# A state-space layer in a fixed instruction order: the kernel transpose moved to the front of a round, tables behind late copies, the next modulation in the first four rounds, gate products in the last two

## The chip, the cores and the metric

One core of one Trainium2 chip runs the whole program. The metric is device time in microseconds of one execution, lower is better. Engines are named as the profile names them: PE (TensorE matmuls), DVE (VectorE), ACT (ScalarE), POOL (GpSimd) and SP (SyncE, which issues the DMA transfers here).

## The reference

A trunk of two residual layers over 512 tokens of width 1024, float32. Layer 0 mixes tokens by a grouped state-space layer (S5), layer 1 by attention with forget gates; a gated convolutional MLP follows each. Every part is modulated by shift, scale and gate from a conditioning vector c. The change touches only the state-space layer:

```python
u = h @ w_in                                  # h: normed, scaled and shifted x
# 64 groups of 16 channels, 64 complex states each, discretised with lam, dt
# scan over time: state = lb * state + bb @ u
y = einsum(hs_re, cr) - einsum(hs_im, ci) + d_skip * u
y = gelu(y)
y = y * sigmoid(y @ w_glu)
return y @ w_out
# the layer's own modulation and the next one's:
shift, scale, gate = split(silu(c) @ ada_w + ada_b, 3)
```

## The kernel before

Weights and activations are float32, and each large product is done as three products of rounded parts (hi by hi, hi by lo, lo by hi). The high part is a copy into a rounded type on ACT (`w_hi`, `a_hi`), the low part a subtraction on POOL or DVE (`w_lo`, `a_lo`, `x_lo`).

The state-space layer is written in method `s5`, in which all engines keep the order of the code: what is written first is issued first on its engine, and an engine that waits holds up all that stands behind it on that engine. There are eight tiles m of 128 channels (8 groups). Time is cut into blocks of 8 steps: inside a block a small convolution kernel does the work, between blocks a scan over 64 blocks. A start stage makes parameters, the scale and shift and the inputs of tiles 0 and 1; then comes a loop of eight rounds. Round m has these steps; the line is that of the kernel before:

- `s5_scan`: 32 small products of `w1` and `u` on PE (L1053), then nine DVE steps with the decay `cf` (made on ACT, L1059) and the turning tables `s_rot`, to the states `ua` (L1081).
- `s5_tables`: POOL builds parts of `s_rot` for later tiles (L966 to L968).
- `s5_columns` of tile m+1: PE products with `dd`, `x` and `s_cd` (L1008, L1011), ACT copies the kernel out as `ktt` (L1016), PE transposes x into `w1` (L1022, copied by ACT at L1023), then PE transposes `ktt` (L1026, "the kernel transpose") and ACT copies it as `kt` (L1027).
- `s5_shifted`: `kt` is stored to DRAM as `s_z` (L1028) and loaded back in shifted form as `tw` (L1037); ACT masks it in eight copies to `t` (L1041).
- `inputs(m+2)`: 24 products on PE (L323), copied by ACT as `uf` (L1313), stored as `s_ud` (L1260) and loaded back turned as `u` (L1264).
- `s5_outputs`: PE products of `u` and `t` (L1091) and of `ua` and `w` (L1100), which ACT sends through a gelu as `yg` (L1106); SP stores it as `s_yd` (L1107). For the gate y is read back as `yt` (L1113), copied by ACT as `a_hi` (L1340), and its low part is `a_lo` (L1344).
- `s5_made`, `s5_states_out`: DVE multiplications (L976) and a POOL addition (L980) that make `x` for tile m+2 and `w` for tile m+1.
- `parted`, `rested`: ACT's high part (L1136) and POOL's low part (L1142) of the input weights of later tiles, loaded as `raw` three at a time.
- `ada_step`: products of c with modulation weights of the next part (L1161), eight steps in all; `ada_columns` (L165, L170) turns their result `ada_rows` into columns. Rows of the layer's own gate are loaded as `ada_raw` and summed on DVE (L265).

In the last two rounds the products of the first four gate tiles (`glu_head`, L1366) stand between these steps; their weights are loaded (`gate_load`), copied (`gate_hi`, L1352) and subtracted (`gate_lo`, L1357) from round 5 on. A fifth gate tile follows, then a loop over the remaining three and `w_out`.

## Time and profile before

| | us |
|---|---|
| median of three runs | 1209.37 |
| the three runs | 1209.37, 1211.93, 1202.32 |
| the profiled execution | 1203.8 |
| its span in the trace | 1201.9 |
| PE, DVE, ACT, POOL busy | 1165.8, 950.2, 649.6, 206.7 |

The span is what the trace covers from the first to the last instruction; the profiled execution took 1.9 us more. PE is busy for 97% of the span. A busy PE is not the same as PE at its best: the trace also gives the clock that TensorE was granted, 1.00 being full speed, and a product takes twice as long at 0.50. In rows of the timeline the number after the start is the duration; matmuls overlap a little, so the distance between two starts is the better measure of what a row takes. In waits, a row says which engine, tile and line waited for which, for how long in total, how often and the longest.

### The profile page before, as it was taken

The numbers are of one execution on the slowest core, as the hardware profiler recorded it, in microseconds if no ns is written. First come the engines' busy times: TensorE is split into PE (matmuls) and PEld (weight loads), VectorE is DVE, ScalarE is ACT, GpSimd is POOL, SyncE is SP. The second block draws the span as 40 slices with busy tenths as digits, with TensorE's granted clock in tenths as the row PEclk, the third lists the DMA queues.
The fourth block names the chain that finished last, engine by engine and source line by source line (L and its number), as shares of the span: only waits on it lengthen the run. The fifth ranks groups of instructions, "written<-read, shape, count | busy, mean of one in ns | idle before, by whom it ended". The sixth has DMA issues, their size and how long they took to land.

```text
span 1201.9 us, 21406 instructions
## 1 busy us (share of the span) xinstructions
PE 1165.8 (97%) x8255; PEld 1038.7 (86%) x8255; DVE 950.2 (79%) x1726; ACT 649.6 (54%) x1169; POOL 206.7 (17%) x266
## 2 busy tenths in 40 slices
PE   7998989999999999999999999999999999999997
PEld 2677767799999999999899788878999999999987
DVE  8865775879898798877676788876899888888855
ACT  3644533435676576666543566664466555555543
POOL 5776540000011111111000433330000000000000
PEclk9898979999999999999999999999999999999999
DMA  9677447853598898998603655622223332333331
GB/s 358 241 244 242 159 151 264 302 171 107 145 249 233 230 255 230 253 239 228 194 25 127 221 180 164 198 97 73 70 87 95 110 126 86 110 124 92 106 88 71
DMA packets 79719, 202.74 MB, mean 169 GB/s; under 512 B 23952, under 2 KB 26480, under 8 KB 78592
## 3 DMA queue, kind: packets, MB, share of 16 engines
q1 hardware_dynamic: 73135, 181.96, 45.1%
q0 software_dynamic: 6192, 18.88, 9.1%
q8 instruction: 65, 1.06, 0.4%
q10 hardware_dynamic: 288, 0.52, 0.1%
q14 instruction: 39, 0.31, 0.1%
HBM read 194.41 MB, written 6.92 MB: 168 GB/s over the span
## 4 chain that ended last, share of the span: by engine, by line
PE 76%; DVE 10%; DMA 6%; ACT 3%; issue 2%; POOL 1%; SPq 0%; DVEq 0%; ACTq 0%; POOLq 0%
PE mmp L323 40%; PE mmp L583 15%; PE aux L583 6%; PE mmp L1582 3%; DMA raw<-in_w_up 2%; DVE w_lo L307 2%; PE aux L1728 2%; PE aux L1711 1%; PE aux L1100 1%; PE aux L1091 1%; DVE ada_raw L265 1%; DVE sums L554 1%; PE aux L1681 1%; DMA yt<-s_yd 1%; DMA raw<-in_s_w_in 1%
## 5 line engine op out<-in xcount | busy, mean ns | idle before, releaser
L302 ACT ACTIVATE w_hi<-raw 128x1024 fp32r<-128x1024 f32 (+4 forms) x196 | 172.1, 887 | 128.6 <-PE mmp L323 55.2
L307 DVE TENSOR_TENSOR w_lo<-raw,w_hi 128x1024 fp32r<-128x1024 f32 (+4 forms) x153 | 155.1, 1016 | 33.0 <-ACT w_hi L302 26.1
L323 PE MATMUL mmp<-ghi,w_hi 128*128 128x512 f32 (+1 forms) x392 | 144.1, 368 | 0.0
L323 PE MATMUL mmp<-glo,w_hi 128*128 128x512 f32 (+1 forms) x392 | 143.7, 367 | 0.0
L323 PE MATMUL mmp<-ghi,w_lo 128*128 128x512 f32 (+1 forms) x392 | 143.6, 366 | 0.0
L323 PE MATMUL mmp<-a_hi,w_hi 128*128 128x256 f32 (+1 forms) x440 | 141.1, 323 | 1.1 <-ACT nm_t L1494 1.1
L323 PE MATMUL mmp<-a_hi,w_lo 128*128 128x256 f32 (+1 forms) x440 | 139.0, 317 | 0.0
L323 PE MATMUL mmp<-a_lo,w_hi 128*128 128x256 f32 (+1 forms) x440 | 138.8, 316 | 0.0
L583 PE MATMUL mmp<-w_hi 128*128 128x256 f32 x420 | 116.6, 278 | 1.6 <-ACT nm_h L590 1.4
L583 PE MATMUL mmp<-w_hi,w_lo 128*128 128x256 f32 x420 | 116.0, 276 | 0.0
L583 PE MATMUL mmp<-w_lo,w_hi 128*128 128x256 f32 x420 | 116.0, 276 | 0.0
L302 ACT ACTIVATE w_hi<-sums 128x1024 fp32r<-128x1024 f32 x78 | 81.8, 1058 | 47.9 <-DVE sums L554 32.3
L307 DVE TENSOR_TENSOR w_lo<-sums,w_hi 128x1024 fp32r<-128x1024 f32 x78 | 94.3, 1218 | 3.1 <-ACT w_hi L302 2.0
L323 PEld LDWEIGHTS mmp<-a_hi,w_hi 128*128 128x128 f32 x440 | 82.2, 188 | 8.6 <-issue 2.5
L265 DVE CUSTOM_DVE_ANT_0 ada_raw<-ada_raw,ada_c,rest 128x1024 f32<-128x1024 f32 x64 | 84.0, 1327 | 5.9 <-DMA ada_raw<-in_ada_rows 5.9
L323 PEld LDWEIGHTS mmp<-a_hi,w_lo 128*128 128x128 f32 x440 | 82.6, 188 | 6.4
L323 PEld LDWEIGHTS mmp<-a_lo,w_hi 128*128 128x128 f32 x440 | 82.8, 188 | 4.6
L323 PEld LDWEIGHTS mmp<-ghi,w_lo 128*128 128x128 f32 x392 | 73.6, 188 | 12.3
L323 PEld LDWEIGHTS mmp<-ghi,w_hi 128*128 128x128 f32 x392 | 73.6, 188 | 11.2
L323 PEld LDWEIGHTS mmp<-glo,w_hi 128*128 128x128 f32 x392 | 73.6, 188 | 11.1
L583 PEld LDWEIGHTS mmp<-w_hi 128*128 128x128 f32 x420 | 78.8, 188 | 2.7 <-ACT nm_h L590 2.7
L554 DVE TENSOR_TENSOR sums<-raw 128x512 f32<-128x512 f32 x70 | 46.0, 686 | 41.5 <-DMA raw<-in_w_up 41.4
(336 smaller groups left out, 3220.9 us busy)
## 6 DMA issues: line engine op xcount, KB each, us to landing
raw<-in_w_up SPq DMA_DIRECT2D x88, 512.0 KB, 3.7
ada_raw<-in_ada_rows SPq DMA_DIRECT2D x64, 512.0 KB, 4.7
raw<-in_ada_w SPq DMA_DIRECT2D x32, 512.0 KB, 6.2
raw<-in_w_down SPq DMA_DIRECT2D x32, 384.0 KB, 4.0
raw<-in_w_down SPq DMA_DIRECT2D x32, 320.0 KB, 3.4
nf<-nfd SPq DMA_DIRECT2D x8, 1152.0 KB, 5.7
w_lo<-in_w_up POOLq DMA_DIRECT2D x17, 512.0 KB, 8.0
raw<-in_fox_qk SPq DMA_DIRECT2D x16, 512.0 KB, 3.3
```

The source lines that it names most:

```text
L265: nc.vector.tensor_tensor_reduce(w, w, self.crow, 1.0, self.ada_b[:, i, m:m + 1], ALU.mult, ALU.add, self.par[i][:, m:m + 1])
L302: nc.scalar.activation(hi, src, AF.Copy)
L307: self.late = (nc.vector.tensor_tensor(lo, src, hi.bitcast(F32), ALU.subtract).ins,)
L323: self.last_mm = self.nc.tensor.matmul(o, wt, xt[:, cols], start=(k == 0 and n == 0), stop=(k == nk - 1 and n == 2),)
L554: sub = lambda o, u, v, op=ALU.subtract: nc.vector.tensor_tensor(o, u, v, op)
L583: self.last_mm = nc.tensor.matmul(o, wt[:, k], xt[:, k], start=(first and k == 0 and n == 0), stop=(k == H - 1 and n == 2), skip_group_che ...
L1091: nc.tensor.matmul(yp[g2][:, k, :], t[:, 2 * k + g2], u[:, g, :], start=(k == 0), stop=False, skip_group_check=True,)
L1100: nc.tensor.matmul(yp[g2][:, k, 1:], w2[rows, k, r].rearrange("p c i -> p (c i)"), st[rows, r, k, :B - 1], start=False, stop=(r == 1), til ...
L1582: self.last_mm = nc.tensor.matmul(ps[q, b][:, :n], xt[:, k, tb], wt, start=(k == 0 and i == 0), stop=(k == KT - 1 and i == 2),)
L1681: nc.tensor.matmul(ps[b][r], q[i][a, tq], kk[j][a, :N], start=(n == 0), stop=(n == 2), tile_position=(64 * r, 0), skip_group_check=True,)
L1711: nc.tensor.transpose(pt[:, r - rs[0], k, :], s[:, r, k * P:(k + 1) * P], self.ident)
L1728: nc.tensor.matmul(pv[:, c * P:], self.v[:, hp, k, r].rearrange("p t d -> p (t d)"), pp[:, r, c + 3 * k:NB + 3 * k, :].rearrange("p b t -> ...
```

## The change

The order of the layer's code is written anew; no product is added or removed.

- Start: the input weights of tile 1 are loaded into a room of `w_hi` ahead of the last modulation loads, and their parts made at once; the columns of tile 0 go ahead of the products with the shift; the states' addition of tile 0 and the low part of w_in(2) go from POOL to DVE; the last of tile 0's tables is built behind them.
- A round: the kernel transpose stands directly behind the columns, ahead of a modulation step and the inputs; `kt` and `tw` are issued ahead of the `u` transfers; `cf` (now `s5_decay`) and `t` of the next tile are made at the end of the round before.
- The eight modulation steps are done in rounds 0 to 3; a row of the gate's modulation is loaded and summed in each of rounds 1 to 4; `ada_columns` moves from round 5 to the tail.
- Last two rounds: the gate products are regrouped (`glu_in`): 12 high-by-high ones in round 6, 36 in round 7. Gate weights are loaded from round 4 on. The low parts of y go to POOL, those of gate tiles 2, 3 and 4 to DVE. The fifth gate tile's products all come last.

```diff
             for m in range(KT):
-                sts[m] = self.s5_scan(m, ws.pop(m), us[m])
+                sts[m] = self.s5_scan(m, ws.pop(m), us[m], cfs.pop(m))
                 next(sts[m])
-                ts[m] = next(ts[m])
...
+                if more:
+                    columns_in(m + 1)
+                    next(cols[m + 1])
...
+                if 0 < m < 4:
+                    ada_step()
+                if m + 4 < KT:
+                    load_w(m + 4)
...
+                if more:
                     ts[m + 1] = self.s5_shifted(m + 1)
                     next(ts[m + 1])
+                if m and m + 2 < KT:
+                    inputs(m + 2)
+                if m + 2 < KT:
+                    turn_u(m + 2)
...
                 outs[m] = self.s5_outputs(m, us.pop(m), ts.pop(m))
                 next(outs[m])
                 outs[m].send((w2s.pop(m), sts.pop(m)))
                 if m + 4 < KT:
                     parted(m + 4)
...
+                if more:
+                    cfs[m + 1] = self.s5_decay(m + 1)
+                    ts[m + 1] = next(ts[m + 1])
                 if steps:
                     ada_step()
```

```diff
+            def glu_in(k, m, j):
+                if m not in gps:
+                    gps[m] = self.mm.tile([P, S], F32, name="mmp")
+                nc.tensor.matmul(gps[m], hi[m][:, k], (yhi, ylo)[j][:, k], start=(k == 0 and j == 0), stop=False)
...
             fifth = [(hi[HEAD][:, k], lo[HEAD][:, k]) for k in range(KT)]
-            for k in range(KT - 1):
-                self.mms(gps[HEAD], fifth, (yhi, ylo), k, KT, full)
             for p in range(2):
                 glu_head(KT - 1, p)
-            self.mms(gps[HEAD], fifth, (yhi, ylo), KT - 1, KT, full)
+            for k in range(KT):
+                self.mms(gps[HEAD], fifth, (yhi, ylo), k, KT, full)
```

Three places show how instructions move. First PE in a round, from the inputs of one round to those of the next. In the kernel before the outputs of round 3 follow the kernel transpose:

```order
L323 MATMUL mmp<-a_xhi,w_lo 128x512
L1026 MATMUL aux<-rest,ktt 128x128
L1091 MATMUL aux<-u,t 128x64 x8
L1100 MATMUL aux<-ua,w_1196 128x63 x16
L1161 MATMUL mmp<-raw,sc_85 32x512 x4
L1053 MATMUL aux<-u,w_1264 64x64 x16
L1008 MATMUL aux<-dd,rest 128x128
L1011 MATMUL aux<-x,s_cd_133 32x128 x8
L1022 MATMUL aux<-rest,x 128x128 x8
L323 MATMUL mmp<-a_xhi,w_hi 128x512
```

In the changed kernel, at the outputs of round 3 as well (lines shift by 1 to 9; L1025 is the kernel transpose, L1062 the scan, L1094 and L1103 the outputs, L1164 a modulation step):

```order
L1094 MATMUL aux<-u,t 128x64 x8
L1103 MATMUL aux<-ua,w_1220 128x63 x16
L1164 MATMUL mmp<-raw,sc_85 32x512 x4
L1062 MATMUL aux<-u,w_1275 64x64 x16
L1007 MATMUL aux<-dd,rest 128x128
L1010 MATMUL aux<-x,s_cd_133 32x128 x8
L1021 MATMUL aux<-rest,x 128x128 x8
L1025 MATMUL aux<-rest,ktt 128x128
```

The kernel transpose has moved from behind the 24 input products to ahead of them. ACT's order around it has stayed: `yg`, `w_hi`, `cf`, `t`, `ktt`, then the copies of `w1`; only `kt` and `uf` behind them have changed places.

Second, SP in a round. Before, in round 4, the `u` transfers of tile 6 come first:

```order
L1260 DMA s_ud<-uf 128x512
L1264 DMA u<-s_ud 128x8x64
L1028 DMA s_z<-kt 128x128
L1037 DMA tw<-s_z 128x1024
L1107 DMA s_yd<-yg 128x8x64
```

In the changed kernel, round 3:

```order
L1027 DMA s_z<-kt 128x128
L193 DMA raw<-in_s_w_in 128x1024
L1036 DMA tw<-s_z 128x1024
L1267 DMA s_ud<-uf 128x512
L1271 DMA u<-s_ud 128x8x64
L258 DMA ada_raw<-in_ada_rows 128x1024
L1110 DMA s_yd<-yg 128x8x64
```

`kt` and `tw` now stand ahead of `uf`'s store and the load that waits for it; a weight load and a modulation row have come in between.

Third, PE in the last two rounds of the changed kernel, from the outputs of round 5 (L1369 are gate products written by `glu_in`):

```order
L1103 MATMUL aux<-ua,w_1554 128x63 x16
L1062 MATMUL aux<-u,w_1616 64x64 x16
L1007 MATMUL aux<-dd,rest 128x128
L1010 MATMUL aux<-x,s_cd_133 32x128 x8
L1021 MATMUL aux<-rest,x 128x128 x8
L1025 MATMUL aux<-rest,ktt 128x128
L1369 MATMUL mmp<-a_hi,w_hi 128x512 x12
L1094 MATMUL aux<-u,t 128x64 x8
L1103 MATMUL aux<-ua,w_1740 128x63 x16
L1062 MATMUL aux<-u,w_1786 64x64 x16
L1369 MATMUL mmp<-a_hi,w_hi 128x512 x4
L1369 MATMUL mmp<-a_lo,w_hi 128x512 x16
```

Before, there stood the modulation columns (L165, L170) ahead of round 6's scan, 16 gate products of high and low parts in turn (L1366) between columns and kernel transpose, and 32 of them behind round 7's scan. In the changed kernel the products of round 6 need no low part of y.

## The prediction

> **What bounds the kernel now.** I read the windows first: busy time in stretches (start:end in us, length, busy us and count of each engine, the clock granted to TensorE, the DMA share, GB/s).

> ```profile
> 40.24:47.08 6.84, 6.84 (x38) 5.63 (x38) 6.84 (x8) 4.99 (x10) 3.06 (x2) 0.50 0.37 113
> 65.05:129.97 64.92, 60.14 (x575) 46.43 (x573) 41.10 (x53) 28.64 (x80) 42.69 (x32) 0.95 0.62 204
> 111.92:118.76 6.84, 6.84 (x71) 4.94 (x69) 0.00 (x0) 2.76 (x7) 5.62 (x8) 0.50 0.48 123
> 129.97:203.14 73.17, 62.03 (x459) 51.84 (x457) 44.89 (x54) 30.53 (x73) 25.73 (x17) 0.86 0.59 200
> 159.72:173.36 13.64, 10.79 (x84) 10.18 (x85) 7.72 (x11) 4.29 (x13) 7.70 (x8) 0.50 0.29 91
> 240.00:1100.00 860.00, 856.99 (x6096) 791.47 (x6095) 707.31 (x1283) 491.44 (x841) 96.54 (x131) 1.00 0.54 157
> ```

> From 240 us on PE is busy 857 of 860 us at full clock, with work the change leaves alone. So the change can only move what lies ahead: the start, rounds 1 to 4 (65.05 to 129.97) and the end of the state-space stage (129.97 to 203.14). There PE loses time in two ways: it waits, and it runs at half clock in spells of 6.84 us (40.24, 111.92; a double one at 159.72). Next, PE's waits in that region:

> ```profile
> PE aux L1026 <- ACT ktt L1016: 4.8, 3, 2.4
> PE aux L1091 <- DVE ua L1081: 4.7, 1, 4.7
> PE aux L1008 <- ACT yg L1106: 2.1, 1, 2.1
> PE mmp L1366 <- ACT a_hi L1340: 1.3, 1, 1.3
> PE mmp L323 <- ACT nm_t L1494: 1.1, 1, 1.1
> ```

> The rounds wait in the kernel transpose (L1026), the last two rounds elsewhere. Then PE's timeline, rows of rounds 0 to 5 (start, duration, instruction, idle before):

> ```profile
> 65.05 1.07 PE L1161 MATMUL mmp<-raw,sc 128*32 128x512 f32 x8
> ...
> 77.59 0.33 PE L1026 MATMUL aux<-rest,ktt 128*128 128x128 f32 x1 [1.66 <-ACT ktt L1016]
> ...
> 109.40 0.33 PE L1026 MATMUL aux<-rest,ktt 128*128 128x128 f32 x1 [2.45 <-ACT ktt L1016]
> 111.57 3.40 PE L1100 MATMUL aux<-ua,w 64*128 64x63 f32 x32
> 114.91 1.94 PE L1161 MATMUL mmp<-raw,sc 128*32 128x512 f32 x8
> 116.77 1.98 PE L1053 MATMUL aux<-u,w 128*64 128x64 f32 x32
> ...
> 126.10 0.27 PE L1026 MATMUL aux<-rest,ktt 128*128 128x128 f32 x1
> 128.04 2.00 PE L1100 MATMUL aux<-ua,w 64*128 64x63 f32 x32
> 129.97 1.07 PE L1161 MATMUL mmp<-raw,sc 128*32 128x512 f32 x8
> 130.96 1.15 PE L1053 MATMUL aux<-u,w 128*64 128x64 f32 x32
> 133.89 0.49 PE L323 MATMUL mmp<-a_xhi,w_hi 128*128 128x512 f32 x1
> 139.48 0.27 PE L1026 MATMUL aux<-rest,ktt 128*128 128x128 f32 x1
> ```

> From these starts, at full clock: a modulation step 0.99; scan products and columns 2.93; inputs 5.59; kernel transpose and outputs 1.94 + 1.93 = 3.87. The spell at 111.92 cost (3.40 - 2.00) + (1.94 - 1.07) + (1.98 - 1.15) = **3.1 us**; it follows the wait of 2.45. Last, ACT:

> ```profile
> 67.50 1.06 ACT L1136 ACTIVATE w_hi<-raw 128x1024 fp32r<-128x1024 f32 x1 [1.68 <-DMA raw<-in_s_w_in]
> ...
> 106.67 2.58 ACT L1041 ACTIVATE t<-tw,rest 128x128 f32<-128x128 f32 x8 [5.93 <-DMA tw<-s_z]
> 109.03 0.31 ACT L1016 ACTIVATE ktt<-aux 128x128 f32<-128x128 f32 x1
> 115.05 0.66 ACT L1106 ACTIVATE yg<-aux 128x256 f32<-128x256 f32 x2 [4.11 <-issue]
> 115.60 1.06 ACT L1136 ACTIVATE w_hi<-raw 128x1024 fp32r<-128x1024 f32 x1
> 116.54 1.27 ACT L1059 ACTIVATE cf<-s_mask,s_mag 128x128 f32<-128x128 f32 x4
> 120.08 2.58 ACT L1041 ACTIVATE t<-tw,rest 128x128 f32<-128x128 f32 x8 [2.27 <-DMA tw<-s_z]
> 122.45 0.32 ACT L1016 ACTIVATE ktt<-aux 128x128 f32<-128x128 f32 x1
> 170.97 1.27 ACT L1059 ACTIVATE cf<-s_mask,s_mag 128x128 f32<-128x128 f32 x4
> 172.14 2.60 ACT L1041 ACTIVATE t<-tw,rest 128x128 f32<-128x128 f32 x8
> ```

> Before, t waits for the load of tw (5.93 us idle), ktt stands behind t, and the transpose behind ktt.

> **Rounds 1 to 4.** The change issues kt and tw ahead of the u transfers and computes t a round later than its load, so t's wait goes. But ACT's own order (yg, w_hi, cf, t, ktt) stays, while PE's transpose moves from behind the inputs to ahead of them: PE now needs ktt 5.59 us earlier. From the end of outputs (call it T; 114.91 above) ACT needs 0.14 to yg, 0.55 to w_hi, 0.94 to cf, 1.17 to t, 2.37 to ktt, and 0.37 from ktt to the transpose (109.03 to 109.40): **T + 5.54**. PE stands there after 0.99 + 2.93 = 3.92 with a modulation step ahead, 2.93 without. What is late next is thus ktt again, by 1.62 us in rounds 2 and 3. In round 4 ada_rows comes in between, a copy of half w_hi's size (some 0.5): 2.1. In round 1 the copy of w_in(4) starts at T + 2.45 as before (67.50, with T 65.05), since its load still follows the subtraction of w_in(3); normal is T + 0.69, so the wait is 3.4. Behind the waiting transpose stand the modulation step, the inputs and the outputs. DVE's scan has those 5.59 us as cover and POOL's tables come early enough: 42.69 of 64.92 us busy. The added row sums lie in DVE's idle time, 41.10 of 64.92 busy.

> A round lasts 5.54 + 0.99 + 5.59 + 3.87 = 15.99; round 4 has no second step, 15.5; round 1 has 1.76 more, 17.75. The sum 65.2 stands against 64.92, before spells: **+0.3**.

> **Spells.** No spell followed the waits of 1.66 (77.59) and 1.3 (a_hi), one followed 2.45. Of rounds 1 to 4, with 3.4, 1.6, 1.6 and 2.1, I count two as spells, the first and one of the others: 2 x 3.1 = **+6.2**; bounds 0 and 12.4.

> **The end.** Round 5, no step and a copy of gate weights in w_hi's place: 5.54 + 5.59 + 3.87 = 15.0 (wait 2.6). Round 6 has no w_hi, so ktt comes 0.94 earlier: 4.60, then 12 gate products, outputs 3.87. Its scan result ua, which cost 4.74 before, is no longer behind DVE's low parts of y (9.69 us for four):

> ```profile
> 147.01 9.69 DVE L1344 TENSOR_TENSOR a_lo<-yt,a_hi 128x512 fp32r<-128x512 f32 x4
> 187.36 6.51 PE L1366 MATMUL mmp<-a_hi,w_lo 128*128 128x512 f32 x28
> 193.71 0.39 PE L323 MATMUL aux<-a_hi,w_hi 128*128 128x512 f32 x1
> ```

> A gate product is (193.71 - 187.36) / 28 = 0.227. Round 6: 4.60 + 2.7 + 3.87 + 0.2 for gate 2's copy = 11.4. Round 7: 1.1 scan, 36 products 8.2, outputs 3.76 = 13.0. That fill covers scan, t and the copies of y. Tail: 72 products 16.3 plus the modulation columns, 1.3 by the row at 36.92 below and their bias, = 17.6; it covers y(7)'s way through DRAM, and the fifth gate, now last, covers the weight copies whose lack left 1.1 idle. Sum **57.0 against 73.17: -16.2**. I count one spell there (round 5's 2.6): **-13.1**; bounds -16.2 and -10.

> POOL trades three full subtractions of weights for seven half-size ones of y, so its 25.73 of 73.17 us hardly grows; its cover is four times enough.

> **The start.**

> ```profile
> 36.92 1.05 PE L170 MATMUL aux<-sel,ada_rows 128*128 128x2 f32 x8 [0.64 <-ACT ada_rows L235]
> 38.78 2.08 PE L1273 MATMUL aux<-par,raw 128*128 128x1 f32 x16
> ...
> L307 DVE TENSOR_TENSOR w_lo<-raw,w_hi 128x1024 fp32r<-128x1024 f32 (+4 forms) x153 | 155.1, 1016 | 33.0 <-ACT w_hi L302 26.1
> ```

> w_in(1) is loaded earlier, so ada_rows no longer stands behind its copy (0.64), and the columns go ahead of the narrow L1273. These narrow rows precede the spell at 40.24. If it goes, half of its 6.84 us is gained, 3.4, the 0.64 in it. If it stays, two full-size passes that move from POOL to DVE (the sum of the states' table and w_lo(2), 1.0 us each by the group of such rows) can push the low parts of x, which the inputs of tile 1 wait for: +1.0. The 2.08 us of near-idle lie between the waits 1.66 and 2.45, so I take the middle: **-1.2**.

> **Sum.** -1.2 + 0.3 + 6.2 - 13.1 = -7.8; the profiled execution took 1203.8: **1196**. That execution lies 5.6 below the median of the three runs (1209.37), inside their 1202.32 to 1211.93. I add nothing for it: my spells are counted by their chance, not as one execution happened to have them. One per cent of the median, 12.1 us, is about what a measurement can tell from no change; 1197.3 is that bound.

> [...] The wait of 2.45 us was followed by half clock (0.50 from 111.92). [...] The sum goes by the row.

> **Rivals.**
> - *Short waits cost no clock.* For: 1.66 did not, and 2.45 is one case. Then only round 1's spell stays: 1203.8 - 1.2 + 0.3 + 3.1 - 16.2 = 1190.
> - *Slower: ktt governs every round.* Place: L1025 behind t on ACT. If each of six rounds draws a spell, three more cost 9.3; if weights come late as in round 1 in two more rounds (each load waits for POOL), 2 x 1.8 = 3.6; and the start keeps its spell, 2.2: 1196 + 15.1 = 1211. It decides from five spells on. Against: the waits of 1.66 and 1.3.
> - *The end does not fill.* If round 6 waits for ua again by 4.7, with one more spell, 7.8 is given back: 1204. Against: DVE has nothing but the scan there.
> - *It doesn't do what it says:* tw still late, because SP is in order and tw stands behind the w_in load that waits for POOL. Then t idles as before; a round gains nothing, and two of them would cost 2.5 each: 1201.

> **How the numbers follow.** Forecast 1196 (two to four spells, 1192 to 1200): 0.5. No clock lost, 1190: 0.2. End unfilled, 1204: 0.12. tw late, 1201: 0.08. Slower, 1211: 0.1. The range 1185 to 1209 leaves out most of the last and the far tails. Below 1197.3 lie the second case and some 0.29 of the first: 0.49. Above 1221.5: 0.03. Between: 0.48.

> **What would show it.** Right: no ACT idle on tw; PE waiting for ktt in the transpose in rounds 1 to 6, some 1.6 to 3.4 each; half-clock spells behind some of them; no wait for ua; from the end of round 4's outputs to the sixth gate tile's first product 57 to 63 us. Wrong: no wait in the transpose (then ACT is quicker than its rows), or waits for POOL's y or weights in rounds 6 and 7.

## The result, and the profile after

| | before | after |
|---|---|---|
| median, us | 1207.95 (8 runs, 1202.32 to 1211.93) | 1197.69 (8 runs, 1192.19 to 1199.56) |
| the profiled execution | 1203.8 | 1199.56 |
| its span | 1201.9 | 1197.8 |

After against before is 0.9913, with a 95% interval of 0.9888 to 0.9939: faster by 0.9%, some 10 us. The two profiled executions differ by less, 4.2, because that of before lies below its median and that of after is the longest of its eight. Readings below compare the two traces; what a run gained or lost is told by medians. Three executions in the experiments (one of the second, two of the third) took 2357 to 4124 us: the medians include them, the ratios do not.

First the changed kernel's windows, in the form of those of before (start:end, length, busy us and count of PE, weight loads, DVE, ACT and POOL, the granted clock, DMA share, GB/s).

```profile
40.24:47.08 6.84, 6.57 (x56) 5.36 (x55) 6.84 (x8) 6.36 (x13) 4.51 (x3) 1.00 0.45 173
64.54:140.14 75.60, 63.36 (x583) 48.12 (x581) 46.18 (x61) 29.00 (x81) 45.09 (x33) 0.91 0.70 234
112.10:115.60 3.50, 3.50 (x12) 2.71 (x9) 2.35 (x4) 0.00 (x0) 0.00 (x0) 0.51 1.08 379
129.00:132.70 3.70, 3.58 (x9) 2.88 (x10) 3.63 (x7) 1.20 (x4) 0.00 (x0) 0.54 0.22 69
140.14:198.89 58.75, 54.96 (x450) 46.75 (x449) 36.57 (x49) 32.22 (x76) 24.38 (x20) 0.97 0.60 195
```

Rounds 1 to 4 (64.54 to 140.14) took 75.60 us against 64.92 before: **+10.7**. From there to the first product of the sixth gate tile it took 58.75 against 73.17: **-14.4**. The start ended 0.5 earlier (64.54 against 65.05), at full clock where before had its half-clock spell. Together -4.2, which is the difference of the two executions: the end paid for everything, and the rounds, whose waits the change rearranged, gave most of it back. (From the first product of the sixth gate tile to the last instruction it took 998.8 us before and 998.9 after.)

PE's waits of the first 215 us and the timeline rows of the kernel transpose in rounds 1 to 6 (in square brackets PE's idle time ahead of the row, and its releaser):

```profile
PE aux L1025 <- ACT ktt L1015: 16.0, 6, 4.3
...
72.96 0.48 PE L1025 MATMUL aux<-rest,ktt 128*128 128x128 f32 x1 [4.25 <-ACT ktt L1015]
...
92.65 0.33 PE L1025 MATMUL aux<-rest,ktt 128*128 128x128 f32 x1 [2.61 <-ACT ktt L1015]
...
110.99 0.33 PE L1025 MATMUL aux<-rest,ktt 128*128 128x128 f32 x1 [3.54 <-ACT ktt L1015]
...
129.12 0.40 PE L1025 MATMUL aux<-rest,ktt 128*128 128x128 f32 x1 [1.84 <-ACT ktt L1015]
...
145.67 0.33 PE L1025 MATMUL aux<-rest,ktt 128*128 128x128 f32 x1 [2.37 <-ACT ktt L1015]
...
161.30 0.33 PE L1025 MATMUL aux<-rest,ktt 128*128 128x128 f32 x1 [1.42 <-ACT ktt L1015]
```

The transpose now waits in all six rounds, 16.0 us in sum, where it waited three times for 4.8; ua and yg are no longer waited for. The waits of rounds 2 and 3 are longer than the 1.62 that ACT's chain explains. The reason stands in ACT's and SP's rows (SP's rows are DMA issues; of the 7.31 us of the modulation loads up to 6.6 are a wait for room, by the last row):

```profile
85.87 1.06 PE L1164 MATMUL mmp<-raw,sc 128*32 128x512 f32 x8
103.29 1.06 PE L1164 MATMUL mmp<-raw,sc 128*32 128x512 f32 x8
...
87.80 1.06 ACT L1139 ACTIVATE w_hi<-raw 128x1024 fp32r<-128x1024 f32 x1 [1.12 <-DMA raw<-in_s_w_in]
...
106.14 1.07 ACT L1139 ACTIVATE w_hi<-raw 128x1024 fp32r<-128x1024 f32 x1 [2.04 <-DMA raw<-in_s_w_in]
...
75.33 7.31 SPq L193 DMA_DIRECT2D raw<-in_ada_w  x2
82.73 0.38 SPq L193 DMA_DIRECT2D raw<-in_s_w_in  x1
...
SPq L193 <- PE mmp L323: 10.3, 2, 6.6
```

Outputs end at 85.87 and 103.29, and w_hi starts 1.9 and 2.9 us behind that, waiting for its load. That load stands on SP behind a modulation load (75.33, 7.31 long) that waits for products of the inputs, L323: its room is the low part of the weights that the inputs of the same round still read.

### The profile page after: what moved, and what is told of

The parts are those of the page before. It is cut to its first block, busy times and chain, and to the rows that moved or that the text cites. A ratio compares the mean times of both kernels' runs of the same rounds, so it can differ in the third digit from the quotient of the medians.

```text
span 1197.8 us, 21400 instructions
## 1 busy us (share of the span) xinstructions
PE 1159.5 (97%) x8255; PEld 1032.8 (86%) x8255; DVE 942.5 (79%) x1724; ACT 649.1 (54%) x1169; POOL 204.8 (17%) x268
## 3 DMA queue, kind: packets, MB, share of 16 engines
q8 instruction: 65, 1.06, 0.4%
## 4 chain that ended last, share of the span: by engine, by line
PE 77%; DVE 8%; DMA 7%; ACT 4%; issue 2%; POOL 1%; SPq 0%; DVEq 0%; ACTq 0%; POOLq 0%
PE mmp L323 41%; PE mmp L583 15%; PE aux L583 6%; PE mmp L1605 3%; DMA raw<-in_w_up 3%; PE aux L1751 2%; DVE w_lo L307 2%; PE aux L1734 1%; DMA raw<-in_s_w_in 1%; DVE sums L554 1%; ACT t L1040 1%; PE mmp L1369 1%; DVE ada_raw L265 1%; PE mmp L1378 1%; PE aux L1704 1%
## 5 line engine op out<-in xcount | busy, mean ns | idle before, releaser
L302 ACT ACTIVATE w_hi<-raw 128x1024 fp32r<-128x1024 f32 (+4 forms) x196 | 171.9, 887 | 114.0 <-PE mmp L323 55.1
L307 DVE TENSOR_TENSOR w_lo<-raw,w_hi 128x1024 fp32r<-128x1024 f32 (+4 forms) x153 | 154.1, 1011 | 31.6 <-ACT w_hi L302 27.8
L323 PE MATMUL mmp<-ghi,w_hi 128*128 128x512 f32 (+1 forms) x392 | 144.1, 368 | 0.0
L323 PE MATMUL mmp<-glo,w_hi 128*128 128x512 f32 (+1 forms) x392 | 143.7, 367 | 0.0
L323 PE MATMUL mmp<-ghi,w_lo 128*128 128x512 f32 (+1 forms) x392 | 143.6, 366 | 0.0
L323 PE MATMUL mmp<-a_hi,w_hi 128*128 128x256 f32 (+1 forms) x440 | 140.9, 323 | 0.0
L323 PE MATMUL mmp<-a_hi,w_lo 128*128 128x256 f32 (+1 forms) x440 | 139.0, 317 | 0.0
L323 PE MATMUL mmp<-a_lo,w_hi 128*128 128x256 f32 (+1 forms) x440 | 138.8, 316 | 0.0
L302 ACT ACTIVATE w_hi<-sums 128x1024 fp32r<-128x1024 f32 x78 | 81.9, 1058 | 53.3 <-DVE sums L554 32.9
L307 DVE TENSOR_TENSOR w_lo<-sums,w_hi 128x1024 fp32r<-128x1024 f32 x78 | 93.9, 1217 | 2.6 <-ACT w_hi L302 2.0
L323 PEld LDWEIGHTS mmp<-a_hi,w_hi 128*128 128x128 f32 x440 | 82.2, 188 | 7.1 <-issue 2.5
L323 PEld LDWEIGHTS mmp<-a_hi,w_lo 128*128 128x128 f32 x440 | 82.6, 188 | 6.4
L323 PEld LDWEIGHTS mmp<-a_lo,w_hi 128*128 128x128 f32 x440 | 82.7, 188 | 4.6
L323 PEld LDWEIGHTS mmp<-ghi,w_lo 128*128 128x128 f32 x392 | 73.6, 188 | 12.3
L323 PEld LDWEIGHTS mmp<-ghi,w_hi 128*128 128x128 f32 x392 | 73.6, 188 | 11.2
L323 PEld LDWEIGHTS mmp<-glo,w_hi 128*128 128x128 f32 x392 | 73.6, 188 | 11.1
```

Source lines behind the costliest of these rows:

```text
L302: nc.scalar.activation(hi, src, AF.Copy)
L307: self.late = (nc.vector.tensor_tensor(lo, src, hi.bitcast(F32), ALU.subtract).ins,)
L323: self.last_mm = self.nc.tensor.matmul(o, wt, xt[:, cols], start=(k == 0 and n == 0), stop=(k == nk - 1 and n == 2),)
```

## The experiments

The ratios are to the kernel before, measured beside it on the same chip (its median there 1208.7 for e1 to e4, 1209.4 for e5 to e8, 1209.2 for e9); 0.9913 is the changed kernel's. Each edit is made to the changed kernel. The experiments are called e1 to e9 in the order in which they stand.

### t behind ktt

```diff
                     cfs[m + 1] = self.s5_decay(m + 1)
-                    ts[m + 1] = next(ts[m + 1])
...
                     next(cols[m + 1])
+                if m:
+                    ts[m] = next(ts[m])
```

> ACT computes the eight parts of t behind ktt, w and kt of the next head group instead of ahead of them; nothing else moves. Theory: the six waits of the kernel transpose (16.0 us together in the changed kernel) come from t standing ahead of ktt on ACT, and the half-clock stretches behind them (some 7 us together: 2.4 + 1.6 + 1.5 + 1.5, by the inputs' lengths in rounds 1, 3, 4 and 5 against round 2) come from those waits. Without t ahead, ktt is 2.4 us earlier: the waits of rounds 2, 4, 5 and 6 go, those of rounds 1 and 3, where the weights' copy is late too, shrink to 1 to 2; about 10 to 12 us of waits and half of the 7 us of clock go: 1180 to 1188. Rival: PE then waits as long for something else (DVE's scan result ua, or u): the sum moves by less than 3 us, 1195 to 1200.

Measured: 1189.28 us, 0.983 (0.9804 to 0.9855). PE's waits in the trace:

```profile
PE aux L1025 <- ACT ktt L1015: 5.3, 2, 2.9
PE mmp L1369 <- ACT w_hi L1359: 3.4, 1, 3.4
```

Four of the six waits are gone; rounds 1 and 3 keep 2.9 and 2.4, where 1 to 2 was expected. A little less was gained than expected, too: in round 6 t now stands ahead of the gate weights' copy, and PE waits 3.4 for that. t ahead of ktt on ACT is shown to be the cause of four of the waits and of a part of the other two.

### The weights' load ahead of the modulation loads

```diff
+                if m + 4 < KT:
+                    load_w(m + 4)
                 if 0 < m < 4:
                     ada_step()
-                if m + 4 < KT:
-                    load_w(m + 4)
```

> The load of w_in for four rounds on is issued ahead of the modulation step's two loads, in rounds 1 to 3; nothing else moves. Theory: in the changed kernel the second load of a modulation step waits on SP for the inputs' products of its own round (6.6 and 3.7 us in rounds 1 and 2), and the w_in load stands behind it, so the copy w_hi starts 1.9 and 2.9 us behind the outputs' end in rounds 2 and 3 instead of 0.7. With the order turned, the waits in the kernel transpose fall from 2.6 to 1.6 in round 2 and from 3.5 to 1.6 in round 3, round 1 keeps its 4.2: 3 us, and up to 1.6 more of half clock: 1193 to 1195. Rival: the weights are late because the DMA engines are full (over 350 GB/s there): the copy starts no earlier, and the time stays within 1 us.

Measured: 1194.17 us, 0.9867 (0.9841 to 0.9892). The interval overlaps that of the changed kernel, so the time alone leaves it open; the trace does not:

```profile
71.50 0.48 PE L1025 MATMUL aux<-rest,ktt 128*128 128x128 f32 x1 [4.39 <-ACT ktt L1015]
...
90.53 0.33 PE L1025 MATMUL aux<-rest,ktt 128*128 128x128 f32 x1 [1.37 <-ACT ktt L1015]
...
106.65 0.33 PE L1025 MATMUL aux<-rest,ktt 128*128 128x128 f32 x1 [1.37 <-ACT ktt L1015]
```

Rounds 2 and 3 now wait 1.4 each instead of 2.6 and 3.5, with no half clock behind (the granted clock is 1.00 from 77.8 to 139.2), and round 1 as long as before. The order on SP is shown to have made what these two waits had above the predicted 1.62, 1.0 and 1.9 us.

### PE kept busy, in the wrong place

```diff
+        for _ in range((0, 0, 30, 18, 25, 12, 16, 9)[m]):
+            nc.tensor.transpose(pk[:, 1], self.ident, self.ident)
         nc.tensor.transpose(pk[:, 1], turned, self.ident)
```

> Ahead of the kernel transpose PE turns the identity matrix 30, 18, 25, 12, 16 and 9 times in rounds 1 to 6 into the place that the transpose then writes: work that adds nothing to the result and lasts about as long as the waits there. The length of the wait for ktt stays, only PE is not idle in it. Theory: the half-clock stretches are the answer to PE's idle time in these waits: they go, and with them some 7 us: 1190 to 1193. Rival: half clock comes from something else in these rounds (what the other engines do, or a fixed rhythm): the stretches and the time stay, 1196 to 1200, or grow by what the added work sticks out.

Measured: 1206.82 us, 0.9977 (0.9961 to 0.9993), 9 us longer than the changed kernel. It tells nothing of its question, as a row of round 1 shows:

```profile
72.87 6.34 PE L1026 MATMUL aux<-rest 128*128 128x128 f32 x30 [5.51 <-ACT ktt L1015]
```

The added work itself waits 5.51 us for ktt: `pk` holds ktt's source too, and the write into its other half came only when ACT had read that. So the work came behind the wait instead of into it.

### The transpose behind the inputs again

```diff
-                    next(cols[m + 1])
...
                 if m and m + 2 < KT:
                     inputs(m + 2)
+                if more:
+                    next(cols[m + 1])
```

(with the store of kt and the load of tw behind it)

> The kernel transpose, its copy, its store and the load of tw stand behind the inputs' products again, where the kernel before had the transpose; all the rest is as in the changed kernel. Theory: the changed place of the transpose alone made the waits of rounds 1 to 6, since ktt is ready 5.5 us behind the outputs' end and PE comes to the transpose at 3.9 ahead of the inputs but at 9.5 behind them: the waits go (16.0), the half clock behind them too (some 7), and the time falls to 1176 to 1186. Rival: tw, loaded 6 us later, is late for t as in the kernel before, ktt stands behind t, and two or three waits of 1.7 to 2.5 come back, each with its half clock: 1188 to 1198.

Measured: 1188.66 us, 0.9823 (0.9798 to 0.9848). The time is the rival's; the trace shows a part of both theories.

```profile
90.17 0.33 PE L1025 MATMUL aux<-rest,ktt 128*128 128x128 f32 x1 [0.93 <-ACT ktt L1015]
...
150.05 0.47 PE L1025 MATMUL aux<-rest,ktt 128*128 128x128 f32 x1 [7.19 <-ACT ktt L1015]
...
147.32 2.57 ACT L1040 ACTIVATE t<-tw,rest 128x128 f32<-128x128 f32 x8 [6.51 <-DMA tw<-s_z]
```

In rounds 1 to 5 no wait reaches 1 us: the changed place of the transpose, with t still ahead of ktt, made them. In round 6, where no inputs stand in between, tw is late as in the rival, t idles for 6.5 us, and PE waits 7.2.

### PE kept busy in the wait

```diff
+                    if 0 < m < KT - 2:
+                        ps = self.mm.tile([P, S], F32, name="mmp")
+                        for _ in range((0, 32, 19, 26, 13, 17)[m]):
+                            nc.tensor.transpose(ps[:, :P], self.ident, self.ident)
                     next(cols[m + 1])
...
-                    inputs(m + 2)
+                    inputs(m + 2, ps)
```

> The fill of e3 in a place where it can run during the wait: ahead of the kernel transpose PE turns the identity matrix 32, 19, 26, 13 and 17 times in rounds 1 to 5 into the tile that the inputs' products overwrite afterwards, and which no engine holds up. It adds nothing to the result. ktt comes as in the changed kernel, so the length of these stretches stays (4.2, 2.6, 3.5, 1.8 and 2.4 us), but PE works in them. Theory: half clock is the answer to PE's idle time there; the half-clock stretches of rounds 1 to 5 go, and with them 5 to 8 us: 1189 to 1193. Rival: half clock comes from something else in these rounds: it stays, and the time with it, 1196 to 1200.

Measured: 1188.89 us, 0.9828 (0.9802 to 0.9853): 9 us less than the changed kernel, for work that serves nothing.

```profile
67.60 3.66 PE L1416 MATMUL mmp<-rest 128*128 128x128 f32 x32
73.86 0.33 PE L1025 MATMUL aux<-rest,ktt 128*128 128x128 f32 x1 [2.60 <-ACT ktt L1015]
...
63.60:134.45 70.85, 67.54 (x672) 54.47 (x670) 46.11 (x61) 29.01 (x81) 43.51 (x32) 1.00 0.75 249
```

From 63.60 to 134.45, rounds 1 to 4, the granted clock is 1.00 (0.91 in the changed kernel); only 2.6 us of idle time are left in round 1, and they drew no half clock. The transpose comes about as late as in the changed kernel: 10.3, 6.5 and 6.8 us behind the outputs' end in rounds 1 to 3, against 8.4, 6.8 and 7.7. So the half clock was the answer to PE's idle time, and with what followed from it it cost 8.8 us, by the medians.

### y's low parts on DVE

```diff
-                        y_lo(nc.gpsimd, n)
+                        y_lo(nc.vector, n)
```

(and so for tiles 4, 5 and 6)

> The low parts of y for gate tiles 0 to 6 are computed on DVE instead of POOL, at the same places of the program. Theory of the prediction: four of them took DVE 9.69 us in the kernel before and kept the scan of round 6 behind them; PE then waits for ua in round 6 by about 4.7 us again, with half clock behind it: 1202 to 1206. Rival: they were slow only because POOL worked beside them; with POOL idle there they take 0.7 us each, 2.8 together, and end ahead of the scan's products: the time stays within 2 us, 1196 to 1200.

Measured: 1196.51 us, 0.9891 (0.9863 to 0.992): no difference from the changed kernel that can be told. The windows of the four subtractions, in the kernel before and in this one:

```profile
147.01:156.70 9.69, 7.11 (x39) 5.47 (x39) 9.69 (x6) 5.68 (x19) 9.14 (x4) 0.70 0.74 222
```

```profile
151.58:154.08 2.50, 2.50 (x41) 2.37 (x42) 2.50 (x5) 1.52 (x3) 0.00 (x0) 1.00 0.31 118
```

With POOL busy for 9.14 of 9.69 us the four took DVE 9.69; with POOL idle they take 2.50 and are done ahead of the scan. The engine they run on did not matter here; that POOL no longer subtracts weights and adds beside them did. A later one of these subtractions in the same run shows it again: it stood beside an addition on POOL and took 2.87, where the next, with POOL idle, took 0.68 (at 173.36).

```profile
164.85 2.87 DVE L1351 TENSOR_TENSOR a_lo<-yt,a_hi 128x512 fp32r<-128x512 f32 x1
164.48 2.69 POOL L980 TENSOR_TENSOR w<-w,x 128x1024 f32<-128x1024 f32 x1 [5.68 <-DVE x L976]
```

### No fill in rounds 6 and 7

```diff
-                    for n in range(3):
-                        for k in range(4):
-                            glu_in(k, n, 0)
...
-            glu_head(6, 0)
+            for k in range(7):
+                glu_head(k, 0)
```

(the 36 products of round 7 likewise)

> The gate products that stand ahead of the outputs of rounds 6 and 7 (12 and 36) are issued in the tail instead, with all other products of the first four gate tiles; the order of every other engine stays. Theory: they fill PE's waits for t and ua. Without them round 6 ends 2.4 us earlier, PE waits some 4.3 us for t and ua in round 7, the outputs of round 7 end at about 175 instead of 181.3, and 48 products of 0.227 us, 10.9, follow in the tail: 4.5 us later, 7.6 with one half-clock stretch: 1202 to 1206. Rival: the tail had idle time of its own that the moved products now fill: 1196 to 1200.

Measured: 1210.0 us, 1.0003 (0.9988 to 1.0018): all of the change's gain is gone.

```profile
PE aux L1094 <- ACT t L1040: 4.1, 1, 4.1
...
166.00:187.00 21.00, 16.91 (x130) 15.67 (x129) 15.47 (x20) 9.01 (x22) 6.41 (x9) 0.52 0.38 114
159.82:214.06 54.24, 48.55 (x320) 41.82 (x318) 26.48 (x36) 22.23 (x51) 11.38 (x13) 0.81 0.60 202
```

The wait for t is the one expected (4.3). What was not expected is the price in clock: from 166 to 187 the mean is 0.52, through the narrow products of both rounds and the wait between them. From the end of round 5's outputs to the sixth gate tile e7 takes 54.24 us, the changed kernel 42.18 (156.71 to 198.89). Rounds 6 and 7 last 24.2 against 24.6, although 10.9 us of products have left them. The fill does two things, it takes the place of the wait and it keeps the clock (1.00 from 166 to 187 in the changed kernel, 0.52 here).

### Nothing ahead of ktt but yg and cf

```diff
                     next(cols[m + 1])
+                if 0 < m < KT - 3:
+                    parted(m + 3)
+                    rested(m + 3)
...
+                if m == KT - 2:
+                    gate_hi(2)
+                if m:
+                    ts[m] = next(ts[m])
```

(the same steps taken out where they stood)

> e1 carried on: in rounds 1 to 5 ACT's copy of the weights w_hi, and t, stand behind ktt, w and kt, and the subtraction that makes w_lo follows its copy; in round 6 the gate weights' copy for tile 2 stands behind ktt and ahead of t. ACT then has yg and cf alone ahead of ktt. Theory: nothing is left that keeps ktt behind PE: no wait in the kernel transpose in rounds 1 to 6, none for w_hi in round 6, hardly any half clock from 64 us on; against e1 that is 2.9 + 2.4 of waits, 3.4 in round 6 and some 8 of half clock: 1170 to 1178. Rival: the weights, copied later, make POOL's subtraction and the next loads late, and PE waits for w_lo or the modulation weights in the inputs: 1184 to 1192.

Measured: 1182.66 us, 0.9772 (0.9742 to 0.9801), the fastest by its median but for the next, which is its equal.

```profile
PE aux L1094 <- ACT t L1040: 2.7, 1, 2.7
PE aux L1010 <- POOL x L980: 2.3, 3, 1.8
...
64.07:123.47 59.40, 58.83 (x583) 44.99 (x581) 42.89 (x59) 30.17 (x81) 39.86 (x30) 1.00 0.84 280
148.28:159.00 10.72, 10.72 (x85) 10.14 (x86) 2.23 (x4) 4.97 (x10) 4.89 (x3) 0.53 0.77 221
```

No wait for ktt is left, and rounds 1 to 4 run at full clock with PE busy for 58.83 of 59.40 us. The time is neither the theory's nor the rival's. Two other waits came up later: 2.7 for t in round 6, where tw's load stood on SP behind gate weights, with half clock from 148.28 on, and 1.8 in round 5 for x, which DVE made late behind a row sum. A part of the rival shows, too: the modulation weights were late in rounds 2 to 4, by 1.2 us in sum. How the shortfall divides among these was not tested.

### tw ahead of the gate weights

```diff
                 if more:
                     ts[m + 1] = self.s5_shifted(m + 1)
                     next(ts[m + 1])
+                if m == KT - 3:
+                    gate_load(3)
+                    gate_load(HEAD)
```

(taken from ahead of it; and `row_sum` behind `s5_made`)

> e8 with two edits for its two remaining waits: in round 5 the load of tw is issued ahead of the last two gate weights' loads on SP, and DVE takes the row sum of rounds 1 to 4 behind the tables x of the round instead of ahead of them. Theory: in e8 PE waited 2.7 us for t in round 6, since tw stood on SP behind those loads, and 1.8 in round 5 for the table x, which DVE began 2.7 us late because its row sum waited for a load; both drew half clock, 5 to 6 us together. All of that goes: 1172 to 1177. Rival: t is late because tw's buffer comes free only when t of the round before has been read, so the wait stays: 1179 to 1184.

Measured: 1181.99 us, 0.9786 (0.9761 to 0.981): e8's time.

```profile
PE aux L1094 <- ACT t L1040: 2.9, 2, 1.6
PE aux L1010 <- POOL x L980: 1.6, 1, 1.6
```

The waits it was made for went, and others of the same sum stand in their place: x in round 6, t in rounds 6 and 7. The time is the rival's, the reason is not. In round 6 t waits for the gate weights' copy ahead of it on ACT, no longer for tw. In round 7 it waits for tw again, but tw's room had long been read: SP issued kt's store at 147.39, behind the loads of y, 8 us after kt was ready. The end looks bound by several chains of about one length, where taking away one shows the next.

## Why the prediction came out right

**What bounds.** The change moved only what lies ahead of 240 us, as the prediction said, and ktt behind t on ACT held PE in rounds 1 to 6 with no idle time of t for tw (the rival in which tw stays late fell with that). e1 and e4 take the waits away from both sides.

**Rounds 1 to 4.** The forecast was 65.2 plus 6.2 for clock, 71.4; measured 75.6. A round with no wait and full clock lasts 14.54 (e8, from the end of round 0's outputs at 64.07 to that of round 1's at 78.61), without a second step 13.37 (e1, round 4): 57.0 for the four. (The kernel before leaves the same: 64.92 less waits of 4.8 and a spell of 3.1.) The waits were 4.25 + 2.61 + 3.54 + 1.84 = 12.24 against 8.74 by the prediction, and 6.4 is left for the clock.

```profile
64.07 1.07 PE L1164 MATMUL mmp<-raw,sc 128*32 128x512 f32 x8
...
78.61 1.39 PE L1164 MATMUL mmp<-raw,sc 128*32 128x512 f32 x8
```

So the term that failed is the **1.62 of rounds 2 and 3**: it let w_hi start 0.69 behind T, because the load had been early enough in the trace of before. The modulation step, moved ahead of the inputs, also moved its two loads on SP, one of them into a room that those inputs still read, and the load of w_in behind it. That queue was not followed; e2 puts it right and gives 1.37. The slower rival had late weights in two more rounds, 3.6 us in sum, but through POOL; the sum was near, the cause another. Round 1 waited 4.25 for 3.4, its copy starting 3.6 behind T instead of 2.45; 0.5 of that is T, which came earlier; why its load took longer than before isn't settled, and e8 makes it harmless.

**Spells.** 6.2 was forecast for two of full price; there were three that cost 2.5, 1.8 and 1.8 (the round's length less 14.54 or 13.37 and its wait), and 0.3 in round 2. The sum is right by luck, as two errors cancel: one spell too few was counted, and each was sized too dear. The 3.1 was read from a stretch of 6.84 us; those of rounds 3 and 4 lasted 3.5 (windows at 112.10 and 129.00), and the one of round 1 lasted 6.83, but PE stood idle in the first 1.75 of it:

```profile
71.21:78.04 6.83, 5.08 (x16) 2.62 (x17) 6.65 (x10) 2.80 (x10) 2.86 (x3) 0.50 0.93 313
```

Each cost about half of the time that PE worked in it: 2.5 of 5.08 us, 1.8 of 3.50 and 1.8 of 3.58. An input product of the changed kernel took 0.43 us from start to start at half clock (112.84 to 113.27) and 0.23 at full clock (116.64 to 116.87), 1.9 times as long, a little less than twice. The prediction's list of spells also leaves out one of the kernel before (146.05 to 152.87); no sum depends on it, since the end was added up from its parts. That idle time made the spells here is shown by e5 (granted clock 1.00 in rounds 1 to 4, against 0.91). That the length of a wait alone decides is not so: 2.61 in round 2 drew none and 1.84 in round 4 drew one, so rival one, for which only round 1 counted, fell; over the runs, waits from 1.42 (e7) to 2.96 (e6) lie on both sides.

**The end.** Forecast 57.0 and a spell of 3.1, 60.1; measured 58.75. By part, from the ends of the outputs: round 5 16.6 (15.0 and a spell, which cost 1.6), round 6 11.4 (11.4), round 7 13.2 (13.0), tail 17.6 (17.6).

```profile
140.14 1.15 PE L1062 MATMUL aux<-u,w 128*64 128x64 f32 x32
156.71 1.15 PE L1062 MATMUL aux<-u,w 128*64 128x64 f32 x32
168.15 1.15 PE L1062 MATMUL aux<-u,w 128*64 128x64 f32 x32
181.30 0.50 PE L1378 MATMUL mmp<-a_hi,w_hi 128*128 128x512 f32 x1
198.89 0.39 PE L323 MATMUL mmp<-a_hi,w_hi 128*128 128x512 f32 x1
```

The sizes were right, but for the spell's, and one reason was not: that the low parts left DVE was not needed for ua's wait to go (e6); on DVE, with POOL at rest, they take 2.50 us and are done in time. That the fill carries the gain is shown by e7, which is 12.3 us longer by its median; in its trace this stretch less round 5 is 12.1 longer.

**The start.** -1.2 forecast, -0.5 measured; half clock at 40.24 went as hoped, and PE then waited for what came next: the inputs of tile 1 for x_lo (0.27), the scan of tile 0 for u (0.61). This term scatters: with the same code round 0 ended at 62.95 in e2 and 64.07 in e8. It wasn't tested by itself.

**The sum.** Against the profiled execution of before -7.8 was forecast, and that of after is 4.2 below it: the rounds were taken 4.2 too cheap, the start 0.7, and the end 1.3 too dear. The median, 1197.69, lies nearer to 1196 than the profiled execution does, because that was the longest of its eight: this is luck. 3.6 us of error in the working stand, not 1.7, and they would be larger had the end not been too dear.

## What to carry to other kernels

Moving a step in a fixed order moves its DMA issues too: follow each one to the room it needs and to who reads that room last, since a load that waits holds the loads behind it (here the w_in load behind 7.31 us of modulation loads on SP). When a consumer is moved ahead, order its producer's engine anew by what is needed first (here ktt before t and before the weights' copy: worth more than the change itself, 1182.7 against 1197.7, where the change gained 10). Where a short wait on PE cannot be taken away, fill it with products that are needed anyway, since the wait cost clock as well as time here (e5: 8.8 us less, clock 1.00 against 0.91 in rounds 1 to 4).

## What the runs showed of the hardware

```profile
88.28:91.69 3.41, 1.76 (x26) 1.23 (x24) 3.20 (x6) 3.41 (x11) 2.38 (x1) 1.00 0.17 59
125.83:129.24 3.41, 1.57 (x26) 1.14 (x18) 3.20 (x6) 3.41 (x12) 1.52 (x1) 1.00 0.45 112
```

  This was read from the traces afterwards; no run was made to test it.
- A stretch of half clock lasted 3.41 us behind 10 of those 13 waits, 6.83 behind the one of 4.25, and 20.48 where narrow products and waits followed each other (e7, 166.89 to 187.37).
- Four subtractions on DVE took 9.69 us beside a busy POOL (9.14 of it, kernel before) and 2.50 beside an idle one (e6); in e6 one took 2.87 beside an addition on POOL and 0.68 without.
